# An attention stage keeps its logits negated and makes the left-block mask a GpSimd select

## The chip, the cores and the metric

The program runs on one core of a Trainium2 chip. The metric is the device time of one execution in microseconds (us), as a median over runs. The engines are named as in the profile: PE is TensorE (PEld its weight load), DVE is VectorE, ACT is ScalarE, POOL is GpSimd, and SP is the engine that issues most loads. L1017 is line 1017 of the kernel before.

## The reference, cut to what matters

Two layers act on a residual stream of 1024 tokens by 1024 channels in float32. The first is a gated MLP with a causal spatial gate over chunks of 128 tokens. The second, to which the change belongs, is sliding-window attention with 16 query heads, 4 shared key and value heads, a bias by distance, and one sink logit per head. A block of 128 queries sees its own block of keys and the one to its left:

```python
def block_fn(args):                      # one block of 128 queries
    i, qb = args
    ...
    logits = jnp.einsum('btkgd,bskd->bkgts', qb, kb).astype(jnp.float32) + alibi
    valid = in_window & ((start - BLOCK + c) >= 0)
    logits = jnp.where(valid, logits, -jnp.inf)
    m = jnp.maximum(jnp.max(logits, axis=-1), sink)
    p = jnp.exp(logits - m[..., None])
    denom = jnp.sum(p, axis=-1) + jnp.exp(sink - m)
    o = jnp.einsum('bkgts,bskd->btkgd', p.astype(vb.dtype), vb).astype(jnp.float32)
    o = o / denom.transpose(0, 3, 1, 2)[..., None]
```

The window is 128 keys, so of the left block a query in row r sees the columns above r, and of its own block the columns up to r. Each query therefore sees exactly 128 keys, one per column index.

## The kernel before

The tokens are worked in two halves of 512. Float32 products are made of three passes: each operand is split into a rounded part (`hi`, a copy on ScalarE, L105) and the rest (`lo`, a subtraction on VectorE, L106), and `mm3` (L167 to L170) issues the three matmuls. Weights are loaded by SP into a ring of three `raw` buffers, some are multiplied by a gain on GpSimd (L140), and then split; `wnext` takes the weight that is due and splits the one behind it, so that a weight is split one tile before its use.

Attention is cut into units: a unit is one block of 128 queries (`b`), one pair of key heads (`p`) and two of the four query heads that share each (`gp`), so four heads of 128 by 128 in a unit, and 16 units in each half. `attn` runs over them, with three stages of three units in flight. In one step it issues `scores` of unit i, `values` of unit i - 2, `transposes` of unit i - 1, some filler, `normalise` of unit i, and filler again. The filler is weight products of other phases: in the first call the projections for z, for keys and values and for q of the second half, in the second call the rest of z and the output projection.

`scores` makes the logits in PSUM (matmuls L997 and L1003). As each query sees one key per column index, the two blocks are merged into one row of 128 logits: a predicated copy with the mask `mrg` (L1008) takes those of the left block where the column is above the row; in the first block (b of 0) it takes -1e30. `tensor_tensor_reduce` (L1013) adds the bias, multiplies by a power of four (the weights of q carry its inverse), writes `pr` to SBUF and leaves the row maximum, begun at the sink logit, in `mx`. The sink logit itself stands as column 129 of `pr` (L986). `nm` is minus the maximum (L1017), and four exps on ScalarE (L1019) use it as their bias and sum their rows into `dn`.

`normalise` inverts `dn` and multiplies (L1025, L1026). `transposes` turns the four tiles on TensorE into the PSUM bank `pt` (L1032). ScalarE copies it to `pc` (L1035), and GpSimd clears in `pc` what does not belong to the unit's own block (an affine select in place, L1036). For b above 0 VectorE multiplies the same PSUM bank by the 0/1 mask `mprev` into `pp`, the left block's part (L1039). `values` multiplies `pc` with the values of the block (L1050) and `pp` with those of the left block (L1053), for two head pairs in turn, into `o`; VectorE multiplies by the gate (`yt`, L1057), which is split into q's place (L1059, helper lines L105 and L106, tiles `q_hi` and `q_lo`).

The pool of these tiles has one buffer for each tag unless it says otherwise. `pr`, `mx`, `nm` and `dn` have two. `pc` has one. `pp` and `yt` share the tag `pp`, and so one buffer, in turn.

The framework plans the order of instructions on each engine and sets the semaphores. An engine runs its own instructions strictly in the planned order, which need not be the order of the source.

Of the kernel before, what the change touches and what calls it, by code (L numbers as in the profile page):

```python
# [7 lines left out]
F32 = mybir.dt.float32  # L8
# [3 lines left out]
AF = mybir.ActivationFunctionType  # L12
ALU = mybir.AluOpType

P = 128
# [15 lines left out]
C_ID, C_BIAS, C_MERGE, C_PREV, C_QS = 0, 128, 640, 768, 896  # L31
# [19 lines left out]
def tile_yoco(  # L51
# [19 lines left out]
    nc = tc.nc  # L71
# [9 lines left out]
    def bank(tag, name):  # L81
        return psum.tile([P, 512], F32, tag=tag, name=name)
# [814 lines left out]
    bp = ctx.enter_context(tc.tile_pool(name="bp", bufs=1))  # L897
    bias = bp.tile([P, 4, P], F32, name="bias")
    nc.sync.dma_start(out=bias.rearrange("p a b -> p (a b)"), in_=consts[:, C_BIAS:C_BIAS + 512])
    mrg = bp.tile([P, P], F32, name="mrg")  # L900
    nc.sync.dma_start(out=mrg, in_=consts[:, C_MERGE:C_MERGE + P])
    mprev = bp.tile([P, P], F32, name="mprev")
    nc.sync.dma_start(out=mprev, in_=consts[:, C_PREV:C_PREV + P])
    neg = bp.tile([P, P], F32, name="neg")
    nc.vector.memset(neg, -1e30)

# [3 lines left out]
    nc.sync.dma_start(out=qsc, in_=consts[:, C_QS:C_QS + 2])  # L910
    snk = bp.tile([P, 4, 4], F32, name="snk")
    nc.sync.dma_start(out=snk.rearrange("p a b -> p (a b)"), in_=sinks.partition_broadcast(P))
    half = [slice(0, 64), slice(64, P)]
    vt = big.tile([P, NB, 256], F32, tag="P1_1", name="vt")

# [59 lines left out]
    class Unit:  # L975
# [4 lines left out]
        def scores(self):  # L980
            b, p, gp, q = self.b, self.p, self.gp, self.q
            bs_ = slice((b % 4) * P, (b % 4 + 1) * P)
            w0 = 0 if b > 0 else P
            pr = bp.tile([P, 4, P + 1], F32, tag="pr", name=f"pr{self.id}", bufs=2)
            mx = bp.tile([P, 2, 2], F32, tag="mx", name=f"mx{self.id}", bufs=2)
            nc.vector.tensor_copy(pr[:, :, P].rearrange("p (a b) -> p a b", a=2),  # L986
                                  snk[:, 2 * p:2 * p + 2, 2 * gp:2 * gp + 2])
            pss = []
            for par in range(2):
                pss.append(bank("s", f"s{self.id}_{par}").rearrange("p (g s) -> p g s", g=2))  # L990
            ks = slice(b * P - P + w0, (b + 1) * P)


            for g in range(2):
                m = p * 4 + gp * 2 + g
                for par in range(2):
                    nc.tensor.matmul(pss[par][:, g, w0:256], lhsT=q[par][:, m, bs_], rhs=kh[par][:, p, ks],  # L997
                                     start=g == 0, stop=False, skip_group_check=True)
            for g in range(2):
                m = p * 4 + gp * 2 + g  # L1000
                for par in range(2):
                    rw = half[par]
                    nc.tensor.matmul(pss[par][:, g, w0:256], lhsT=q[par][rw, m, bs_], rhs=kl[rw, p, ks],  # L1003
                                     start=False, stop=g == 1, skip_group_check=True)
            for par in range(2):
                ps = pss[par]
                c = ps[:, :, P:256]
                nc.vector.copy_predicated(c, mrg.bitcast(U32).unsqueeze(1).broadcast_to([P, 2, P]),  # L1008
                                          ps[:, :, 0:P] if b > 0 else neg.unsqueeze(1).broadcast_to([P, 2, P]))
                kv = 2 * p + par  # L1010
                for g in range(2):
                    gg = 2 * gp + g
                    nc.vector.tensor_tensor_reduce(pr[:, 2 * par + g, 0:P], c[:, g], bias[:, gg], 4.0 ** -kv,  # L1013
                                                   snk[:, kv, gg:gg + 1], ALU.add, ALU.max, mx[:, par, g:g + 1])
            nm = bp.tile([P, 2, 2], F32, tag="nm", name=f"nm{self.id}", bufs=2)
            dn = bp.tile([P, 2, 2], F32, tag="dn", name=f"dn{self.id}", bufs=2)
            nc.vector.tensor_scalar(nm, mx, -1.0, None, ALU.mult)  # L1017
            for i in range(4):
                nc.scalar.activation(pr[:, i], pr[:, i], AF.Exp, bias=nm[:, i // 2, i % 2:i % 2 + 1],  # L1019
                                     accum_out=dn[:, i // 2, i % 2:i % 2 + 1])  # L1020
            self.pr, self.dn = pr, dn

# [6 lines left out]
        def transposes(self):  # L1029
            pt = bank("s", f"pt{self.id}")  # L1030
            for i in range(4):
                nc.tensor.transpose(pt[:, i * P:(i + 1) * P], self.pr[:, i, 0:P], ident)  # L1032
            ptv = pt.rearrange("p (a b) -> p a b", a=4)
            self.pc = pc = bp.tile([P, 4, P], F32, tag="pc", name=f"pc{self.id}")
            nc.scalar.activation(pc, ptv, AF.Copy)  # L1035
            nc.gpsimd.affine_select(pc, pc, [[0, 4], [1, P]], ALU.is_ge, 0.0, base=0, channel_multiplier=-1)  # L1036
            if self.b > 0:
                self.pp = bp.tile([P, 4, P], F32, tag="pp", name=f"pp{self.id}")
                nc.vector.tensor_tensor(self.pp, ptv, mprev.unsqueeze(1).broadcast_to([P, 4, P]), ALU.mult)  # L1039

        def values(self):
            b, p, gp, q, z = self.b, self.p, self.gp, self.q, self.z
# [186 lines left out]
```

## Time and profile before

| what | us |
| --- | --- |
| median of 3 runs (lowest, highest) | 1073.43 (1072.39, 1078.94) |
| the profiled execution, its time | 1077.21 |
| the profiled execution, its span from first to last instruction | 1075.5 |

The profile covers one execution. Busy time of an engine does not count issue, waiting or semaphores; matmuls overlap one another and their weight loads. A window gives the busy time of each engine in a stretch of the span, and the clock that TensorE was granted there as a share of full speed. In a timeline a row can stand for several like instructions in a row (x2, x4), and the brackets give the idle time of the engine before it and what ended it.

### The profile page before, as it was taken

What the parts mean: (1) busy time and instruction counts of PE and PEld (TensorE: products, weight loads), DVE (VectorE), ACT (ScalarE), POOL (GpSimd) and SP (SyncE); (2) the same over time, 40 slices, a digit from 0 to 9 for tenths busy, and PEclk for the clock granted to TensorE, in tenths of its full rate; (3) what the DMA queues carried; (4) which work ended last, traced back from release to release, by engine and by line L of the source; (5) the groups of instructions that cost most, each with busy time, mean ns of one, the idle gap of its engine ahead of it and who ended that gap; (6) DMA issues with size and microseconds to landing.
All of it is one profiled execution on the core that took longest, in us unless ns stands there. A gap on an engine that the chain in (4) does not pass through costs nothing.

```text
span 1075.5 us, 14187 instructions
## 1 busy us (share of the span) xinstructions
PE 1051.4 (98%) x5108; PEld 859.1 (80%) x5108; DVE 781.6 (73%) x1335; ACT 582.7 (54%) x983; POOL 282.3 (26%) x199
## 2 busy tenths in 40 slices
PE   9999999999999999999999999999999989999997
PEld 7887778888888888888878878788778767777775
DVE  6987456867767767767795896746768985778873
ACT  7684444555565565555445464536675455675631
POOL 0000023254253443531561211313212323200120
PEclk9999999999999999999999999999999999999999
DMA  8787243334334333448968633724111212112353
GB/s 299 267 274 261 96 158 107 117 117 139 113 108 139 126 117 113 145 142 281 353 239 289 195 118 105 263 98 157 59 59 60 79 53 85 59 59 79 119 176 117
DMA packets 68709, 159.75 MB, mean 149 GB/s; under 512 B 6176, under 2 KB 16800, under 8 KB 68640
## 3 DMA queue, kind: packets, MB, share of 16 engines
q1 hardware_dynamic: 63744, 150.37, 41.0%
q10 hardware_dynamic: 4896, 8.48, 2.2%
q8 instruction: 40, 0.66, 0.3%
q14 instruction: 29, 0.24, 0.1%
HBM read 127.37 MB, written 31.46 MB: 148 GB/s over the span
## 4 chain that ended last, share of the span: by engine, by line
PE 79%; DVE 11%; ACT 3%; issue 2%; DMA 2%; POOL 2%; DVEq 0%; POOLq 0%; ACTq 0%
PE ub L168 5%; PE ub L170 5%; PE ub L169 5%; PE ob L168 5%; PE ob L169 5%; PE ob L170 5%; PE qz L168 4%; PE qz L170 4%; PE qz L169 4%; PE uc L168 3%; PE uc L170 3%; PE uc L169 3%; PE sp L592 3%; PE vb L168 2%; PE vb L169 2%
## 5 line engine op out<-in xcount | busy, mean ns | idle before, releaser
L140 POOL TENSOR_TENSOR raw_w<-raw_w,gn 128x1024 f32<-128x1024 f32 x32 | 66.4, 2076 | 186.2 <-DMA raw_w<-in_wqz_dram 164.7
L168 PE MATMUL qz<-n_hi,whi 128*128 128x512 f32 x256 | 102.8, 402 | 0.1
L170 PE MATMUL qz<-n_hi,wlo 128*128 128x512 f32 x256 | 100.8, 394 | 1.2 <-DVE wlo L106 1.2
L169 PE MATMUL qz<-n_lo,whi 128*128 128x512 f32 x256 | 100.4, 392 | 0.0
L106 DVE TENSOR_TENSOR wlo<-raw_w,whi 128x1024 fp32r<-128x1024 f32 x40 | 57.7, 1443 | 32.0 <-ACT whi L105 28.7
L1036 POOL TENSOR_SCALAR_AFFINE_SELECT pc<-pc 128x512 f32<-128x512 f32 x32 | 24.9, 779 | 151.9 <-ACT pc L1035 151.9
L105 ACT ACTIVATE whi<-raw_w 128x1024 fp32r<-128x1024 f32 x40 | 42.2, 1055 | 34.6 <-PE qz L169 15.4
L105 ACT ACTIVATE uzhilo_g<-f 128x1024 fp32r<-128x1024 f32 x31 | 32.9, 1060 | 50.0 <-PE uc L170 42.6
L170 PEld LDWEIGHTS qz<-n_hi,wlo 128*128 128x128 f32 x256 | 48.4, 189 | 11.9 <-DVE wlo L106 1.6
L168 PEld LDWEIGHTS qz<-n_hi,whi 128*128 128x128 f32 x256 | 48.5, 189 | 10.8 <-ACT pr L1019 0.4
L169 PEld LDWEIGHTS qz<-n_lo,whi 128*128 128x128 f32 x256 | 48.6, 190 | 9.5
L106 DVE TENSOR_TENSOR uzhilo_g<-f,uzhilo_g 128x1024 fp32r<-128x1024 f32 x31 | 39.0, 1257 | 21.9 <-ACT uzhilo_g L105 21.9
L205 POOL TENSOR_TENSOR f<-raw_uz,raw_uz 128x512 f32<-128x512 f32 x16 | 21.5, 1343 | 125.3 <-DVE uzhilo_g L106 125.3
L1019 ACT ACTIVATE pr<-pr,nm 128x129 f32<-128x129 f32 x128 | 49.8, 392 | 8.0 <-DVE nm L1017 5.4
L205 POOL TENSOR_TENSOR f<-raw_uz 128x512 f32<-128x512 f32 x16 | 20.6, 1291 | 126.6 <-DMA raw_uz<-in_wuz_in_dram 71.7
L208 ACT ACTIVATE uz_slots<-ub 128x512 f32<-128x512 f32 x48 | 28.4, 591 | 43.6 <-PE ub L170 41.5
L168 PE MATMUL ub<-T,whi_g 128*128 128x512 f32 x128 | 50.6, 396 | 0.0
L168 PE MATMUL ub<-T,uzhilo_g 128*128 128x512 f32 x128 | 50.5, 394 | 0.0
L170 PE MATMUL ub<-T,wlo_g 128*128 128x512 f32 x128 | 49.9, 390 | 0.0
L170 PE MATMUL ub<-T,uzhilo_g 128*128 128x512 f32 x128 | 49.9, 390 | 0.0
L169 PE MATMUL ub<-T,whi_g 128*128 128x512 f32 x128 | 49.8, 389 | 0.0
L169 PE MATMUL ub<-T,uzhilo_g 128*128 128x512 f32 x128 | 49.8, 389 | 0.0
(316 smaller groups left out, 3287.7 us busy)
## 6 DMA issues: line engine op xcount, KB each, us to landing
raw_uz<-in_wuz_in_dram SPq DMA_DIRECT2D x32, 512.0 KB, 3.5
raw_w<-in_wqz_dram SPq DMA_DIRECT2D x32, 512.0 KB, 3.5
td<-uz_slots SPq DMA_DIRECT2D x56, 256.0 KB, 2.0
orawP2a<-td SPq DMA_DIRECT2D x28, 512.0 KB, 4.5
raw<-in_wv_in_dram SPq DMA_DIRECT2D x17, 512.0 KB, 4.9
orawP2b<-in_wo_a_dram SPq DMA_DIRECT2D x17, 512.0 KB, 6.2
vg<-vd SPq DMA_DIRECT2D x8, 1024.0 KB, 5.4
raw_o<-in_wo_a_dram SPq DMA_DIRECT2D x15, 512.0 KB, 5.4
```

The source lines that it names most:

```text
L105: nc.scalar.activation(hi, src, AF.Copy)
L106: nc.vector.tensor_tensor(lo, src, hi.bitcast(F32), ALU.subtract)
L140: nc.gpsimd.tensor_tensor(rv, rv, g, ALU.mult)
L168: nc.tensor.matmul(out, lhsT=a_hi, rhs=b_hi, start=start, stop=False, skip_group_check=True)
L169: nc.tensor.matmul(out, lhsT=a_hi, rhs=b_lo, start=False, stop=False, skip_group_check=True)
L170: nc.tensor.matmul(out, lhsT=a_lo, rhs=b_hi, start=False, stop=stop, skip_group_check=True)
L205: (eng or nc.vector).tensor_tensor(out, a, b, op)
L208: nc.scalar.activation(out, a, AF.Copy)
L592: nc.tensor.matmul(psv[:, n], lhsT=d["vg"][:, 4 * j + n, i * P:(i + 1) * P], rhs=d["wc"], start=True, stop=True)
L1019: nc.scalar.activation(pr[:, i], pr[:, i], AF.Exp, bias=nm[:, i // 2, i % 2:i % 2 + 1], accum_out=dn[:, i // 2, i % 2:i % 2 + 1])
L1036: nc.gpsimd.affine_select(pc, pc, [[0, 4], [1, P]], ALU.is_ge, 0.0, base=0, channel_multiplier=-1)
```

## The change

The sinks are multiplied by -1 once, when they are loaded. `tensor_tensor_reduce` multiplies by minus the power of four and reduces with the minimum, so that `pr`, its sink column and `mx` hold negated logits. The exps take a factor of -1 and `mx` itself as bias; the negation into `nm` is gone from each unit, and its tile too. The mask `mprev` and its load are gone. In place of VectorE's product from PSUM, GpSimd makes `pp` by an affine select from `pc`, the copy in SBUF, ahead of the in-place select that clears the rest of `pc`.

```diff
-    mprev = bp.tile([P, P], F32, name="mprev")
-    nc.sync.dma_start(out=mprev, in_=consts[:, C_PREV:C_PREV + P])
...
+    nc.vector.tensor_scalar(snk, snk, -1.0, None, ALU.mult)
...
-                    nc.vector.tensor_tensor_reduce(pr[:, 2 * par + g, 0:P], c[:, g], bias[:, gg], 4.0 ** -kv,
-                                                   snk[:, kv, gg:gg + 1], ALU.add, ALU.max, mx[:, par, g:g + 1])
-            nm = bp.tile([P, 2, 2], F32, tag="nm", name=f"nm{self.id}", bufs=2)
+                    nc.vector.tensor_tensor_reduce(pr[:, 2 * par + g, 0:P], c[:, g], bias[:, gg], -(4.0 ** -kv),
+                                                   snk[:, kv, gg:gg + 1], ALU.add, ALU.min, mx[:, par, g:g + 1])
             dn = bp.tile([P, 2, 2], F32, tag="dn", name=f"dn{self.id}", bufs=2)
-            nc.vector.tensor_scalar(nm, mx, -1.0, None, ALU.mult)
             for i in range(4):
-                nc.scalar.activation(pr[:, i], pr[:, i], AF.Exp, bias=nm[:, i // 2, i % 2:i % 2 + 1],
+                nc.scalar.activation(pr[:, i], pr[:, i], AF.Exp, bias=mx[:, i // 2, i % 2:i % 2 + 1], scale=-1.0,
                                      accum_out=dn[:, i // 2, i % 2:i % 2 + 1])
...
             nc.scalar.activation(pc, ptv, AF.Copy)
-            nc.gpsimd.affine_select(pc, pc, [[0, 4], [1, P]], ALU.is_ge, 0.0, base=0, channel_multiplier=-1)
             if self.b > 0:
                 self.pp = bp.tile([P, 4, P], F32, tag="pp", name=f"pp{self.id}")
-                nc.vector.tensor_tensor(self.pp, ptv, mprev.unsqueeze(1).broadcast_to([P, 4, P]), ALU.mult)
+                nc.gpsimd.affine_select(self.pp, pc, [[0, 4], [-1, P]], ALU.is_ge, 0.0, base=-1, channel_multiplier=1)
+            nc.gpsimd.affine_select(pc, pc, [[0, 4], [1, P]], ALU.is_ge, 0.0, base=0, channel_multiplier=-1)
```

## Rows read from the trace of the kernel before

**Rows 1.** The page, part 1: busy us of an engine, its share of the span, and its instructions.

```profile
PE 1051.4 (98%) x5108; PEld 859.1 (80%) x5108; DVE 781.6 (73%) x1335; ACT 582.7 (54%) x983; POOL 282.3 (26%) x199
```

**Rows 2.** Windows by stage: the stretch and its length, then busy us of each engine (with the number of its instructions), the granted clock, the share of the DMA engines and GB/s. The first is the first attention call with the rest of its filler, the second the second call.

```profile
745.00:890.00 145.00, 139.03 (x776) 109.04 (x775) 113.10 (x309) 90.82 (x222) 38.34 (x30) 0.99 0.22 70
...
905.00:1035.00 130.00, 130.00 (x709) 100.11 (x707) 101.24 (x309) 83.82 (x215) 23.15 (x22) 1.00 0.28 93
```

**Rows 3.** Windows of 5 us within the first attention call, with the same columns (PE, PEld, DVE, ACT, POOL, clock, DMA share, GB/s).

```profile
860.00:865.00 5.00, 3.11 (x18) 2.25 (x18) 3.47 (x9) 4.56 (x12) 0.16 (x1) 0.90 0.00 0
865.00:870.00 5.00, 5.00 (x18) 3.96 (x18) 4.70 (x17) 1.97 (x9) 0.64 (x1) 0.76 0.20 56
...
880.00:885.00 5.00, 3.88 (x20) 2.70 (x21) 4.18 (x8) 4.77 (x13) 0.96 (x1) 1.00 0.01 3
```

**Rows 4.** Waits of TensorE from 640 us to the end: who waited for whom, us in total, times, the longest.

```profile
PE pt L1032 <- DVE pr L1026: 3.2, 3, 1.9
PE o L1053 <- DVE pp L1039: 2.0, 2, 1.7
```

**Rows 5.** Views of one line or tile each, the row of its instructions: count, then nanoseconds of one (least, median, most), first and last start, and the shapes.

```profile
L1036 POOL TENSOR_SCALAR_AFFINE_SELECT pc<-pc x32: 637/637/1609, 756.5 to 1029.4; 128x512 f32<-128x512 f32 x32
...
L1039 DVE TENSOR_TENSOR pp<-pt,mprev x28: 676/691/692, 767.7 to 1031.2; 128x512 f32<-128x512 f32 x28
...
L1017 DVE TENSOR_SCALAR nm<-mx x32: 153/161/1765, 751.3 to 1022.1; 128x4 f32<-128x4 f32 x32
...
L1013 DVE CUSTOM_DVE_ANT_0 pr<-s,bias,snk x128: 337/347/353, 750.1 to 1021.4; 128x128 f32<-128x128 f32 x128
...
L1026 DVE TENSOR_TENSOR pr<-pr,dn x32: 678/692/1589, 753.4 to 1026.6; 128x512 f32<-128x512 f32 x32
...
L106 DVE TENSOR_TENSOR q_lo<-yt,q_hi x32: 410/426/855, 767.2 to 1038.4; 128x256 fp32r<-128x256 f32 x32
```

**Rows 6.** Groups by line and shape on VectorE, 745 to 1040 us: count, busy us, mean nanoseconds of one, idle time before them.

```profile
L1026 DVE TENSOR_TENSOR pr<-pr,dn 128x512 f32<-128x512 f32 x32 | 23.7, 740 | 0.9
...
L1039 DVE TENSOR_TENSOR pp<-pt,mprev 128x512 f32<-128x512 f32 x28 | 19.3, 688 | 0.6
...
L1017 DVE TENSOR_SCALAR nm<-mx 128x4 f32<-128x4 f32 x32 | 10.5, 328 | 0.1
```

**Rows 7.** The timeline around 858 to 863 us: start, us, engine, line, operation.

```profile
858.26 1.90 POOL L140 TENSOR_TENSOR raw_w<-raw_w,gn 128x1024 f32<-128x1024 f32 x1 [2.70 <-DVE mx L1013]
858.42 1.76 DVE L1017 TENSOR_SCALAR nm<-mx 128x4 f32<-128x4 f32 x1
858.54 0.42 ACT L105 ACTIVATE q_hi<-yt 128x256 fp32r<-128x256 f32 x1 [2.40 <-DVE yt L1057]
...
860.28 0.40 ACT L1019 ACTIVATE pr<-pr,nm 128x129 f32<-128x129 f32 x1 [1.32 <-DVE pr L986]
...
863.01 0.41 PE L1032 MATMUL pt<-ident,pr 128*128 128x128 f32 x2 [1.89 <-DVE pr L1026]
```

**Rows 8.** The timeline of five units: the q_lo subtraction of the unit before on VectorE, and TensorE's value products (L1050 from pc, L1053 from pp); for the first of them also the pc select on GpSimd.

```profile
801.00 0.91 POOL L1036 TENSOR_SCALAR_AFFINE_SELECT pc<-pc 128x512 f32<-128x512 f32 x1 [11.90 <-ACT pc L1035]
...
801.00 0.42 DVE L106 TENSOR_TENSOR q_lo<-yt,q_hi 128x256 fp32r<-128x256 f32 x1
...
801.96 0.43 PE L1050 MATMUL o<-pc,vt 128*64 128x256 f32 x1 [0.19 <-POOL pc L1036]
...
841.79 0.41 DVE L106 TENSOR_TENSOR q_lo<-yt,q_hi 128x256 fp32r<-128x256 f32 x1
...
842.81 0.61 PE L1050 MATMUL o<-pc,vt 128*64 128x256 f32 x2
...
850.93 0.43 DVE L106 TENSOR_TENSOR q_lo<-yt,q_hi 128x256 fp32r<-128x256 f32 x1 [0.33 <-ACT q_hi L105]
...
851.14 0.65 PE L1050 MATMUL o<-pc,vt 128*64 128x256 f32 x2
...
852.13 0.43 PE L1053 MATMUL o<-pp,vt 128*64 128x256 f32 x1 [0.35 <-DVE pp L1039]
...
878.67 0.65 PE L1050 MATMUL o<-pc,vt 128*64 128x256 f32 x2
...
879.80 0.41 DVE L106 TENSOR_TENSOR q_lo<-yt,q_hi 128x256 fp32r<-128x256 f32 x1
...
880.99 0.43 PE L1053 MATMUL o<-pp,vt 128*64 128x256 f32 x1 [1.67 <-DVE pp L1039]
...
987.33 0.42 DVE L106 TENSOR_TENSOR q_lo<-yt,q_hi 128x256 fp32r<-128x256 f32 x1
...
987.77 0.43 PE L1050 MATMUL o<-pc,vt 128*64 128x256 f32 x1
```

**Rows 9.** The timeline of GpSimd: the weight multiply that follows the pc select in two of these units.

```profile
838.82 1.90 POOL L140 TENSOR_TENSOR raw_w<-raw_w,gn 128x1024 f32<-128x1024 f32 x1
...
848.54 1.90 POOL L140 TENSOR_TENSOR raw_w<-raw_w,gn 128x1024 f32<-128x1024 f32 x1
```

**Rows 10.** The timeline of VectorE where the sink logits come in (the copies into pr of the first two units, and the next instruction).

```profile
652.44 0.24 DVE L986 COPY pr<-snk 128x4 f32<-128x4 f32 x2 [2.29 <-DMA snk<-in_sinks_dram]
654.72 1.29 DVE L106 TENSOR_TENSOR n_lo<-nt,n_hi 128x512 fp32r<-128x512 f32 x2 [2.04 <-ACT n_hi L105]
```

## The prediction, made before the change was run

> **What bounds the kernel now.** I read the page's busy shares first: TensorE is busy 1051.4 of 1075.5 us, VectorE 781.6 [rows 1]. So work taken from another engine pays only where TensorE stands idle. The windows by stage say where the change can reach: the first attention call with what is left of its filler (745 to 890 us) has TensorE busy 139.0 of 145.0, so 6.0 us idle at a mean granted clock of 0.99; the second call (905 to 1035 us) has it busy in all 130.0 [rows 2]. The fine windows of the first call show where the 6.0 us lie: 1.89 us in 860 to 865, 1.12 us in 880 to 885, and behind the first of these the granted clock reads 0.90 and 0.76 [rows 3], a mixture of the 2.4 GHz level with some time at 1.2. Those two stretches cost 5 x 0.10 + 5 x 0.24 = 1.7 us of clock. The pause of 1.67 us at 879 to 881 [rows 8] left the clock at 1.00 [rows 3]. The waits of TensorE name two releasers that the change touches: pt (the transposes) on pr, 3.2 us in 3 waits, and o (the value products) on pp, 2.0 us in 2 [rows 4].
>
> **The change, part by part.** VectorE loses nm, 32 x 0.328 = 10.5 us, and pp, 28 x 0.688 = 19.3 us: 29.8 us in all, of which a unit loses 0.16 + 0.69 = 0.85 us at the medians [rows 5, 6]. As TensorE is the bound, this is not the gain.
>
> Removing nm takes a link out of maximum, nm, exp. Its median is 0.161 us, its longest 1.765 [rows 5]. The long ones are waits: at 858.42 nm ran until 860.18, while GpSimd's weight multiply ran from 858.26 to 860.16; the first exp began at 860.28, and the transposes at 863.01 after 1.89 us of idle TensorE [rows 7]. Without nm the first exp follows the q_hi copy on ScalarE, which ends at 858.96: 1.3 us earlier, so are the transposes, and 1.89 - 1.3 leaves a pause of 0.6, shorter than the 1.67 that cost no clock. **Term 1: -1.3 us; term 2: -1.7 us of clock.** Ends of both together: 0, if the sink copy or q_lo that stand behind nm are held in its place and something needs them; and -7.7, if all idle time (6.0) and the clock (1.7) come back. I take -3.0, since only this wait hangs on nm alone.
>
> The select for pp on GpSimd: the shape is that of the pc select, min and median 0.637, longest 1.609 [rows 5]; nothing in the tensor differs but the pattern, so I take 0.64. It cannot start with the ScalarE copy alone. pp and yt share one buffer (tag pp, one deep), so it also waits for the last reader of the unit before's yt, the q_lo subtraction on VectorE. That held for VectorE's pp too; new is that the in-place pc select stands behind it in GpSimd's queue. Formerly pc was ready early, and the four pc products could run before pp was there. Now both come at q_lo's end + 0.05 (a handoff such as from 801.91, the end of the select, to the product at 801.96) + 2 x 0.64 = 1.33 us. Of the 28 units with a left block five are then late by VectorE's old times: q_lo ends at 801.42, 842.20, 851.36, 880.21 and 987.75, their products began at 801.96, 842.81, 851.14, 878.67 and 987.77 [rows 8], so 0.79 + 0.72 + 1.55 + 2.87 + 1.31 = 7.2 us. Two of these already waited 0.35 and 1.67 for pp [rows 8], which leaves 5.2. The other 23 come out in time, their cover being the filler's weight products between the copy and the value products. VectorE's 0.85 us relief stands ahead of q_lo; taken off each, 0, 0, 0.35, 0.35 and 0.46 remain. **Term 3: +1.2 us**, ends 0 and +5.2. Behind the waiting select on GpSimd stands the next weight multiply: in the unit of 842 it ran at 838.82, in that of 851 at 848.54 [rows 9]; behind a select pair that ends at 843.53 and 852.69 they would come 4.7 and 4.1 us later, and ScalarE's split of that weight after them. I cost this at nothing, because weights are split one tile ahead of use; without that cover it is up to 8.8 us.
>
> The lock: nm (0.153 to 1.765), pr's normalisation (0.678 to 1.589) and q_lo (0.410 to 0.855) sometimes run long; the old pp, which read PSUM, never did (0.676 to 0.692) [rows 5]. So work that is never held moves to the engine that holds others, 28 x 0.64 = 17.9 us of it. The Trainium skill (SBUF — State Buffer, Who interferes with whom) states that a VectorE instruction with two SBUF inputs contends with a GpSimd instruction that reads SBUF, and that the later one is blocked for the whole of the first. The trace agrees in which rows run long. By that rule at its fullest the relief shrinks from 29.8 to 11.9 us, and the sum turns to no gain (rival below). Sized by rows: the normalisation's mean is 0.740 against a minimum of 0.678 [rows 5, 6] with 32 selects about, so 0.06 us each; on the path it matters in the 3 waits for pr. **Term 4: +0.2 us**, ends 0 and 3 x 0.64 = 1.9.
>
> The negation of the sinks adds one VectorE instruction of 16 elements a row, once, between 0.15 us (the smallest small-tile row, nm) and 1.77 (nm held). It stands where VectorE waits 2.29 us for the sinks and then 2.04 us for ScalarE [rows 10]: 0, and without that cover its own length. One load on SP goes, ahead of that of the sinks, and gates nothing else. Exp with a factor of -1 and the reduction by minimum have the shapes of before; the trace has no row with a factor or a minimum there, and a cost either way is bounded by the spread of the existing row, 0.337 to 0.353 over 128 of them [rows 5], 2 us of VectorE: 0 on the path.
>
> The sum: -1.3 - 1.7 + 1.2 + 0.2 = -1.6 us. The profiled execution took 1077.21 us (span 1075.5 and 1.7 around it), so 1075.6. It lies 3.78 above the median of the three runs, 1073.43; against that I forecast 1071.8.
>
> **The rivals.** (a) The select pair on GpSimd comes late and the waiting moves there. For it: the five late units; against it: 23 units have room and VectorE runs ahead. Price: +5.2 with nothing of terms 1 and 2 gained, 1078.6; with the two delayed weight multiplies coming through in full +14.0, 1087.4. It decides over 1% (10.7 us) from 0.38 us of lateness in each of 28 units. (b) The lock eats the relief: term 4 at its end of 1.9 and term 3 without the relief's help in the two units that waited already (2 x 0.85 = 1.7 more), so -3.0 + 2.9 + 1.9 = +1.8, 1075.2; for it speak the long rows, against it the small mean. This is the page's rule named above. (c) All idle time of the first call and its clock come back: -7.7, 1065.7. For it: in 840 to 885 VectorE is the engine that TensorE waits for; against it: part of the idle time hangs on ScalarE's exps and on q_lo. (d) The change does not do what it says: the instructions are planned in another order on the engines (the order is not that of the source: the sink copies of the first two units ran at 652.44 [rows 10], far ahead of their scores), and this outweighs it. Its size has no row; I give it a gain over 1% only, losses being in (a).
>
> **How the numbers follow.** Forecast 0.47, from 0 to -4 us; (a) 0.22, of which 0.08 beyond +10.7; (b) 0.13; (c) 0.15; (d) 0.03. The predicted time is the forecast's. The range goes from (c), 1065, to beyond (a)'s first price, 1081; it leaves out (a)'s tail, (d) and some of the stretch between, under 0.2. The forecast's own range is 1069 to 1074. About 1% is what a measurement of this kernel can tell from no change: faster 0.03 is (d), slower 0.08 is (a)'s tail, the rest is within.
>
> **What would show it.** Right: the wait of pt on pr in the first call falls below 2 us and no window of 860 to 870 shows a clock under 0.95; VectorE's busy time falls by 25 to 30 us, GpSimd's rises by 18 to 22; o waits on GpSimd (pc or pp) in two to five units for 1 to 3 us. Wrong: o waiting on GpSimd for more than 5 us, the second call no longer at full TensorE, weight multiplies starting later and ScalarE's split waiting for them (a); the normalisation's mean over 0.9 us (b); all idle time gone (c); another order of the filler on TensorE (d).

## The result, and the profile after

| | before | after |
| --- | --- | --- |
| median of the runs, us (lowest, highest) | 1074.72 (1072.39, 1078.94), 14 runs | 1079.93 (1077.11, 1086.08), 14 runs |
| the profiled execution, its time, us | 1077.21 | 1077.78 |
| its span, us | 1075.5 | 1076.0 |

The ratio is 1.0048, 95% interval 1.0035 to 1.0061: the change costs 5.2 us (3.8 to 6.6). The forecast was a gain of 1.6 us. The time lies inside the range and within 1%, but on the other side of no change.

One caution for reading the two profiles: that of before lies 2.5 us above its median, that of after 2.2 below, so their spans differ by 0.5 us only. What follows is read from the attention stretch. From the first score product to the last value product it took 287.9 us before (746.78 to 1034.70) and 291.1 after (744.78 to 1035.85), which is 3.2 us more, with TensorE idle 6.0 and 11.3 us of it.

The page of after, part 1 (busy us, share, instructions), to be read against [rows 1]:

```profile
PE 1047.3 (97%) x5108; PEld 855.7 (80%) x5108; DVE 765.3 (71%) x1276; ACT 581.6 (54%) x983; POOL 304.0 (28%) x227
```

GpSimd rose by 21.7 us. VectorE fell by 16.3 only, though the instructions taken from it had held 29.8. The windows of after, in the columns of [rows 2]:

```profile
745.00:890.00 145.00, 135.12 (x765) 106.36 (x764) 103.27 (x280) 90.33 (x222) 47.33 (x41) 0.99 0.18 66
905.00:1035.00 130.00, 128.54 (x700) 99.19 (x698) 93.57 (x278) 83.08 (x216) 35.36 (x39) 1.00 0.26 93
```

TensorE's idle time grew from 6.0 to 9.9 us in the first call and from 0 to 1.5 in the second: 5.4 us together. The waits of TensorE from 640 us to the end, those that answer to [rows 4], tell who ended it:

```profile
PE o L1048 <- POOL pc L1037: 10.2, 7, 2.7
PE pt L1030 <- DVE pr L1024: 1.1, 2, 0.8
```

The value products now wait for `pc` on GpSimd, 10.2 us in 7 waits, where before they waited 0.2 us for `pc` and 2.0 for `pp`. Transposes wait 1.1 instead of 3.2. Net, the waits grew by 10.0 - 2.0 - 2.1 = 5.9 us, near the 5.3 by which idle time grew. They are not the whole account, as the stretch grew by 3.2 only. Most of the rest is in the value products themselves, which were busy for less time after. The busy time of TensorE on the tile `o`, first before and then after:

```profile
740.00:1050.00 310.00, 35.88 (x240) 0.99 0.26 86
740.00:1050.00 310.00, 34.04 (x240) 0.99 0.24 84
```

The step from these 3.2 us to the 5.2 of the medians can only be estimated. Both profiled executions have a mean granted clock of 0.997; over all runs it is 0.9944 after, and 0.9958 in the 78 runs of the kernel before beside the experiments. The difference is about 1.5 us of the span. So on the mean after lost more clock, which the two profiles don't show.

Who is waited for on the other engines, 745 to 1040 us, after:

```profile
POOL pp L1036 <- DVE q_lo L106: 97.5, 20, 9.2
...
ACT pr L1017 <- DVE mx L1012: 33.2, 19, 4.1
...
ACT pc L1033 <- PE pt L1030: 25.0, 13, 4.4
```

and the same view of before for ScalarE:

```profile
ACT pc L1035 <- PE pt L1032: 41.6, 22, 4.2
...
ACT pr L1019 <- DVE nm L1017: 5.4, 5, 1.9
```

Two things are to be seen. In 20 of its 28 units GpSimd's new select starts when `q_lo` releases the shared buffer, not when ScalarE's copy is there. And ScalarE waits at another place: before, mostly for the transposes ahead of the `pc` copy (22 times), rarely for `nm` ahead of the exps (5); after, 19 times for the maximum ahead of the exps. Its planned order has changed. Of the 28 steps that have all three, the `pc` copy and `q_hi` mostly run ahead of the exps before (27 and 24 times); after, `q_hi` runs behind the exps in all 28 and the `pc` copy in 18. VectorE followed: `q_lo` comes ahead of the step's normalisation 25 times before and 7 after. The order on TensorE is nearly the same.

One step of after shows the whole chain, in the timeline from 866 to 873 us (start, us, engine, line, operation, idle time before it):

```profile
866.62 0.40 ACT L1017 ACTIVATE pr<-pr,mx 128x129 f32<-128x129 f32 x1 [1.27 <-DVE mx L1012]
...
867.49 1.90 POOL L140 TENSOR_TENSOR raw_w<-raw_w,gn 128x1024 f32<-128x1024 f32 x1 [6.14 <-DMA raw_w<-in_wqz_dram]
867.60 1.82 DVE L985 COPY pr<-snk 128x4 f32<-128x4 f32 x1
...
868.18 0.40 ACT L105 ACTIVATE q_hi<-yt 128x256 fp32r<-128x256 f32 x1
...
869.52 0.69 DVE L1024 TENSOR_TENSOR pr<-pr,dn 128x512 f32<-128x512 f32 x1
870.13 0.42 DVE L106 TENSOR_TENSOR q_lo<-yt,q_hi 128x256 fp32r<-128x256 f32 x1
...
870.47 1.22 DVE L106 TENSOR_TENSOR wlo<-raw_w,whi 128x1024 fp32r<-128x1024 f32 x1
...
870.68 1.50 POOL L1036 TENSOR_SCALAR_AFFINE_SELECT pp<-pc 128x512 f32<-128x512 f32 x1 [1.30 <-DVE q_lo L106]
...
872.25 0.63 POOL L1037 TENSOR_SCALAR_AFFINE_SELECT pc<-pc 128x512 f32<-128x512 f32 x1
...
872.94 1.13 PE L1048 MATMUL o<-pc,vt 128*64 128x256 f32 x4 [2.15 <-POOL pc L1037]
```

The exps go first on ScalarE, so `q_hi` comes behind them. On VectorE the sink copy is held for 1.82 us beside GpSimd's weight multiply, as `nm` was before [rows 7], and the normalisation stands ahead of `q_lo`. `q_lo` ends at 870.55, `pp` is selected (held for 1.50, beside VectorE's split of a weight), then `pc`, and TensorE has stood still for 2.15 us. From these rows the shares can be estimated: `q_hi` was there at 868.58, so `q_lo` is 1.55 us late. Without the hold the normalisation would have followed the last exp (its sum is read by 868.28) and ended near 869.1; that makes 0.5 by its place and 1.0 by the held copy. The held select adds 1.50 - 0.63 = 0.87.

Two more of the seven waits show what else made the pair late:

```profile
816.68 0.42 DVE L106 TENSOR_TENSOR q_lo<-yt,q_hi 128x256 fp32r<-128x256 f32 x1
816.90 1.96 POOL L140 TENSOR_TENSOR raw_w<-raw_w,gn 128x1024 f32<-128x1024 f32 x1 [4.97 <-DVE pr L1024]
818.82 0.63 POOL L1036 TENSOR_SCALAR_AFFINE_SELECT pp<-pc 128x512 f32<-128x512 f32 x1
819.51 0.63 POOL L1037 TENSOR_SCALAR_AFFINE_SELECT pc<-pc 128x512 f32<-128x512 f32 x1
820.20 0.66 PE L1048 MATMUL o<-pc,vt 128*64 128x256 f32 x4 [1.46 <-POOL pc L1037]
...
843.47 0.42 DVE L106 TENSOR_TENSOR q_lo<-yt,q_hi 128x256 fp32r<-128x256 f32 x1
844.01 1.23 DVE L106 TENSOR_TENSOR wlo<-raw_w,whi 128x1024 fp32r<-128x1024 f32 x1
844.02 1.72 POOL L1036 TENSOR_SCALAR_AFFINE_SELECT pp<-pc 128x512 f32<-128x512 f32 x1 [1.30 <-DVE q_lo L106]
845.80 0.70 POOL L1037 TENSOR_SCALAR_AFFINE_SELECT pc<-pc 128x512 f32<-128x512 f32 x1
846.56 0.66 PE L1048 MATMUL o<-pc,vt 128*64 128x256 f32 x4 [2.73 <-POOL pc L1037]
```

In the first, a weight multiply stands ahead of the pair in GpSimd's queue; in the second, the select is held for 1.72 us beside the split of a weight. The seven value products that waited began at 784.87, 803.88, 820.20, 846.56, 872.94, 936.11 and 1028.11, and the time from the end of `q_lo` to them was 1.85, 1.91, 3.10, 2.68, 2.39, 1.52 and 2.73 us, where two selects at 0.64 and a handoff would be 1.33.

The fine windows of after, columns of [rows 3]:

```profile
845.00:850.00 5.00, 3.44 (x21) 2.59 (x22) 4.89 (x15) 2.33 (x7) 2.56 (x3) 1.00 0.29 105
...
865.00:870.00 5.00, 5.00 (x27) 4.08 (x25) 4.85 (x14) 3.23 (x11) 1.90 (x1) 1.00 0.25 97
870.00:875.00 5.00, 2.85 (x15) 1.24 (x12) 4.85 (x14) 1.51 (x3) 2.13 (x2) 0.75 0.27 105
875.00:880.00 5.00, 5.00 (x23) 4.25 (x24) 2.85 (x7) 2.56 (x10) 2.14 (x2) 0.91 0.00 0
```

The pause at 860 to 863 is gone and its loss of clock too, but the new pause brings one back: 5 x 0.25 + 5 x 0.09 = 1.7 us, as much as before. The longest pause, 2.73 us up to 846.56, cost no clock.

The rows of one line or tile each, after, with count and least, median and longest nanoseconds, beside [rows 5]:

```profile
L985 DVE COPY pr<-snk x32: 135/164/1816, 650.2 to 1015.9; 128x4 f32<-128x4 f32 x32
...
L1036 POOL TENSOR_SCALAR_AFFINE_SELECT pp<-pc x28: 630/635/1715, 767.4 to 1032.4; 128x512 f32<-128x512 f32 x28
```

and two groups on VectorE, 745 to 1040 us, in the columns of [rows 6]:

```profile
L1024 DVE TENSOR_TENSOR pr<-pr,dn 128x512 f32<-128x512 f32 x32 | 24.3, 761 | 0.9
...
L985 DVE COPY pr<-snk 128x4 f32<-128x4 f32 x30 | 13.1, 438 | 0.5 <-PE pt L1030 0.5
```

The sink copy's mean was 0.176 us before (5.3 us for the 30 copies): it grew by 7.8 us. `nm` had stood 5.3 us above its median (10.5 - 32 x 0.161), so as much as its hold, and some more, is found again here.

### The profile page after: what moved, and what is told of

Read it like the earlier page. It is cut to its first block, busy times and chain, and to the rows that moved or that the text cites. A ratio compares the mean times of both kernels' runs of the same rounds, so it can differ in the third digit from the quotient of the medians.

```text
span 1076.0 us, 14195 instructions
## 1 busy us (share of the span) xinstructions
PE 1047.3 (97%) x5108; PEld 855.7 (80%) x5108; DVE 765.3 (71%) x1276; ACT 581.6 (54%) x983; POOL 304.0 (28%) x227
## 4 chain that ended last, share of the span: by engine, by line
PE 81%; DVE 9%; ACT 4%; POOL 2%; issue 2%; DMA 1%; SPq 0%; POOLq 0%; DVEq 0%; ACTq 0%
PE ub L170 5%; PE ub L168 5%; PE ub L169 5%; PE ob L168 5%; PE ob L169 5%; PE ob L170 5%; PE qz L168 4%; PE qz L169 4%; PE qz L170 4%; PE uc L170 3%; PE uc L169 3%; PE uc L168 3%; PE sp L592 3%; PE vb L169 2%; PE vb L170 2%
## 5 line engine op out<-in xcount | busy, mean ns | idle before, releaser
L1017 ACT ACTIVATE pr<-pr,mx 128x129 f32<-128x129 f32 x128 | 50.0, 393 | 33.4 <-DVE mx L1012 33.2
L1036 POOL TENSOR_SCALAR_AFFINE_SELECT pp<-pc 128x512 f32<-128x512 f32 x28 | 23.0, 822 | 123.5 <-DVE q_lo L106 97.5
```

The source lines that it names most:

```text
L1017: nc.scalar.activation(pr[:, i], pr[:, i], AF.Exp, bias=mx[:, i // 2, i % 2:i % 2 + 1], scale=-1.0, accum_out=dn[:, i // 2, i % 2:i % 2 + 1])
L1036: nc.gpsimd.affine_select(self.pp, pc, [[0, 4], [-1, P]], ALU.is_ge, 0.0, base=-1, channel_multiplier=1)
```

## The experiments

Four theories were open after the result. **Order:** without `nm` the plan of ScalarE changes (exps first), and this makes `pc` and `q_lo` late. **Shared buffer:** the `pp` select waits in GpSimd's queue for the buffer that `yt` holds until `q_lo`, and the `pc` select stands behind it. **Negation:** negated logits cost something themselves. **Lock:** more work on GpSimd holds VectorE, or is held by it. Ratios are to the kernel before, run beside each on the same chip, with 95% intervals.

**The negation alone** (the mask stays on VectorE):

```diff
+    nc.vector.tensor_scalar(snk, snk, -1.0, None, ALU.mult)
...
-            nc.vector.tensor_scalar(nm, mx, -1.0, None, ALU.mult)
...
-                nc.scalar.activation(pr[:, i], pr[:, i], AF.Exp, bias=nm[:, i // 2, i % 2:i % 2 + 1],
+                nc.scalar.activation(pr[:, i], pr[:, i], AF.Exp, bias=mx[:, i // 2, i % 2:i % 2 + 1], scale=-1.0,
```

> One part of the change alone: logits negated and nm gone, pp still VectorE's product from PSUM. The plan of ScalarE is the one of the full change (exps, then q_hi, then the pc copy). Theory O (the lost time needs both parts: without nm the planner puts the exps of a unit ahead of the pc copy and of q_hi, which makes both some 2 us later, and the two selects on GpSimd in a row then come too late): -2 to +1.5 us against before, since the pc copy had 4 to 5 us of room and VectorE's pp does not hold pc back; TensorE's wait of o on GpSimd's pc stays under 2 us. Theory B (the selects and the shared buffer alone, whatever ScalarE's order): -1 to -3 us. Theory N (the order of ScalarE alone costs it): +4 to +6 us.

Measured: 1074.37 us, ratio 0.9978 (0.9964 to 0.9993), -2.4 us. Waits of TensorE from 745 us on, and the window of the first call:

```profile
PE o L1052 <- DVE pp L1038: 1.7, 3, 0.7
PE o L1049 <- POOL pc L1035: 1.3, 2, 1.1
PE pt L1031 <- DVE pr L1025: 0.3, 1, 0.3
```

```profile
745.00:890.00 145.00, 141.91 (x791) 111.27 (x791) 110.63 (x298) 92.31 (x224) 39.56 (x30) 1.00 0.21 73
```

The wait for `pr` falls from 3.2 to 0.3, the clock in this window is 1.00, idle time halves to 3.1. So the negation gains by itself, although its ScalarE order is that of after, exps first. The gain is a little above the range that the order theory gave. Outside this stretch the profiled execution did lose clock (0.73 at 635 to 640 us and 0.92 at 640 to 645), as much as before lost at 860 to 870 [rows 3].

**The select alone** (`nm` stays):

```diff
-                nc.vector.tensor_tensor(self.pp, ptv, mprev.unsqueeze(1).broadcast_to([P, 4, P]), ALU.mult)
+                nc.gpsimd.affine_select(self.pp, pc, [[0, 4], [-1, P]], ALU.is_ge, 0.0, base=-1, channel_multiplier=1)
+            nc.gpsimd.affine_select(pc, pc, [[0, 4], [1, P]], ALU.is_ge, 0.0, base=0, channel_multiplier=-1)
```

> The other part alone: pp as a select on GpSimd from pc, logits and nm as before. The plan of ScalarE is the one of before (pc copy, q_hi, exps). Theory O: +0 to +2.5 us against before, o waiting on GpSimd's pc for 2 to 5 us, as the five late units of the prediction say. Theory B: +5 to +7 us, o waiting on GpSimd for about 10 us as in the full change. Theory L (the lock between GpSimd and VectorE): +4 to +7 us with the normalisation's mean well above 0.74 us. Theory N: within 1 us of before.

Measured: 1079.92 us, ratio 1.0028 (1.0009 to 1.0047), +3.0 us. ScalarE keeps the order of before. Two waits, 745 to 1040 us:

```profile
POOL pp L1036 <- DVE q_lo L106: 65.8, 14, 10.0
...
PE o L1048 <- POOL pc L1037: 7.2, 5, 1.9
```

The select loses even in the old order, through `q_lo`, and by an amount between the ranges of the two theories. The parts add up to -2.4 + 3.0 = +0.6 us; together they cost 5.2. The rest, some 4.6 us (by the three intervals give or take 2.9), belongs to neither part alone.

**The full change with ScalarE's order held to `pc` copy, `q_hi`, exps:**

```diff
+        def exps(self):
...
+            if i < len(units):
+                with ExitStack() as s:
+                    if i > 0:
+                        s.enter_context(tc.issue_after(units[i - 1].ci))
+                    if i > 1:
+                        s.enter_context(tc.issue_after(units[i - 2].qi))
+                    units[i].exps()
```

> The full change with ScalarE's order pinned by plan-only edges to that of before: in each step the exps are issued behind the pc copy and q_hi. Theory O: the pc copy and q_lo are early again, o waits on GpSimd under 5 us, the time is 3 to 6 us below the full change, so -1 to +2 us against before. Theories B and L: as the full change, +4 to +6 us against before.

Measured: 1076.17 us, ratio 0.9997 (0.9983 to 1.0011). The wait for `pc` falls to 5.5 us in 3 (from 10.2 in 7), not quite under 5. The order is worth about 5.5 us here (0.9997 against 1.0048).

**The kernel before with the order of after, strictly:**

```diff
+                with ExitStack() as s:
+                    if i < len(units):
+                        s.enter_context(tc.issue_after(units[i].ei))
+                    units[i - 2].values()
...
+                with ExitStack() as s:
+                    if i >= 2:
+                        s.enter_context(tc.issue_after(units[i - 2].qi))
+                    units[i - 1].transposes()
```

> The kernel before with ScalarE's order pinned to that of the full change (exps, q_hi, pc copy); nothing else differs. Theory O: the order alone is mostly hidden by the 4 to 5 us of room of pc, 0 to +2.5 us against before. Theory N: +4 to +6 us. Theory B: within 1 us of before.

Measured: 1087.53 us, ratio 1.0105 (1.0082 to 1.0128), +11.3 us: far more than any theory gave it. ScalarE's exps wait for `nm`, with `q_hi`, the `pc` copy and the splits behind them (waits of ScalarE, 745 to 1040 us; before 5.4 us in 5):

```profile
ACT pr L1020 <- DVE nm L1018: 35.8, 13, 4.9
```

That this wait makes the 11.3 us is not shown. The planned order on TensorE changed too, far more than in after, and its value products were busy for 42.5 us here against 35.9 before. What the pin does on TensorE was not separated from what it does on ScalarE, so the run can't size the order in after.

**The kernel before with its own order pinned** (`pc` copy, `q_hi`, exps, by the lines of the pin above), a control:

> The kernel before with ScalarE's order pinned to pc copy, q_hi, exps in every step; its plan had that order in 25 or so of its 32 steps already. A control for the runs with the pin: if the pin's gain there (0.9953 for the negation with the pin against 0.9978 without) is one of order alone, this run falls too, by 1 to 3 us. If it needs the negation, within 1 us of before, as nm keeps the exps late anyway.

Measured: 1077.20 us, ratio 1.0004 (0.9986 to 1.0023). The pin itself costs and gains nothing clear of the noise; as the plan had this order in most steps already, it changes little here.

**The full change, with a buffer of its own for `yt`** (the constant -1e30 is kept as one column to make room, which changes no value):

```diff
-    neg = bp.tile([P, P], F32, name="neg")
+    neg = bp.tile([P, 1], F32, name="neg")
...
-            yt = bp.tile([P, 2, P], F32, tag="pp", name=f"yt{self.id}")
+            yt = bp.tile([P, 2, P], F32, tag="yt", name=f"yt{self.id}")
```

> The full change, but yt has a buffer of its own in place of sharing that of pp (room for it comes from keeping the constant of -1e30 as one column that is broadcast, used in the 2 x 4 units of the first block). pp's select then waits for the pc copy alone and not for q_lo of the unit before; ScalarE's order stays that of the full change. Theory S (the shared buffer makes the pair of selects late, and the order hurts because it makes q_lo late): GpSimd's wait on q_lo goes from 97.5 us to nothing, o waits on GpSimd under 3 us, and the time is 4 to 7 us below the full change: -2 to +1 us against before. Theory P (the late pc copy itself does it, with or without q_lo): +3 to +5 us against before.

Measured: 1072.56 us, ratio 0.9966 (0.9951 to 0.9982), -3.7 us, more than the shared-buffer theory forecast (-2 to +1). The one-column constant that comes with it is no cause: the eight copies that use it took 3.5 us after and 3.4 here. GpSimd's select now waits for ScalarE's copy, in no unit for `q_lo`:

```profile
POOL pp L1036 <- ACT pc L1033: 123.7, 24, 11.0
```

TensorE still waits 4.2 us for `pc` in 5 waits: the copy comes behind the exps.

**The select alone with that buffer:** the two diffs above together.

> The select part alone (nm kept, plan's order of before), with yt in its own buffer. Theory S: the buffer is what the select part lost by (it measured 1.0028 alone), so -1 to -4 us against before. If the select on GpSimd is itself the loss: +2 to +4 us, as without the buffer.

Measured: 1072.03 us, ratio 0.9975 (0.9958 to 0.9991), where the select alone gave 1.0028. The shared buffer is what the select alone lost by.

**The full change with the buffer and the pinned order:**

> The full change with both mends: yt in its own buffer, and ScalarE's order pinned to pc copy, q_hi, exps. Theory S: like the run with the buffer alone, -3 to 0 us against before. Theory P: no better than the pin alone, which measured 0.9997 of before: -1 to +1 us. If the lock between GpSimd's selects and VectorE costs what rival (b) said, neither mend goes below 0 us.

Measured: 1070.00 us, ratio 0.9939 (0.9921 to 0.9957), -6.6 us, beyond the forecast of -3 to 0. Its windows, columns of [rows 2]:

```profile
745.00:890.00 145.00, 143.00 (x809) 114.18 (x809) 109.71 (x287) 93.61 (x227) 46.98 (x42) 1.00 0.21 73
905.00:1035.00 130.00, 130.00 (x697) 100.00 (x696) 93.12 (x273) 78.16 (x207) 33.86 (x37) 1.00 0.29 102
```

and what is left of the waits that the change touches:

```profile
PE pt L1034 <- DVE pr L1028: 2.1, 4, 0.9
```

No value product waits for GpSimd, and 4.0 of the first call's 6.0 us of idle time and its loss of clock are back. Yet VectorE's holds are longer here than in either kernel (mean of the normalisation, columns of [rows 6]):

```profile
L1028 DVE TENSOR_TENSOR pr<-pr,dn 128x512 f32<-128x512 f32 x32 | 27.6, 863 | 1.0
```

This beats both kernels, before by 0.6% and, by the two ratios, after by 1.1%.

**The negation alone with the pinned order:**

> Negated logits without nm, pp on VectorE as before, ScalarE's order pinned to pc copy, q_hi, exps. It asks whether the gain of the negation alone (0.9978 of before) hangs on the order that comes with it. Theory S: no, with one select a unit and pp on VectorE pc has room in either order, -1 to -4 us against before. If the order of exps first was itself the gain: within 1 us of before.

Measured: 1071.40 us, ratio 0.9953 (0.9936 to 0.9970). That is -5.1 us, beyond the range of -1 to -4. Two things follow. The order costs something without the select too: 0.9978 with the exps first, 0.9953 without, 2.7 us, though hardly more than the noise of the two (give or take 2.4). And the run does not differ from the one above by more than the intervals: that the select on GpSimd adds to the negation, even with both mends, is not shown.

The ratios so far, side by side:

| | `nm` kept, order of before | negation, order of after | negation, order held |
| --- | --- | --- | --- |
| `pp` on VectorE | 1 | 0.9978 | 0.9953 |
| select on GpSimd, shared buffer | 1.0028 | 1.0048 | 0.9997 |
| select on GpSimd, buffer for `yt` | 0.9975 | 0.9966 | 0.9939 |

Down each column, the select with the shared buffer costs 0.3 to 0.7%, and with a buffer for `yt` it costs nothing; in the first column it gains 0.3%. From the second column to the third, the order costs 0.3% in the first and the last row and 0.5% where the buffer is shared.

**The same as the best version, with `pc` selected first:**

```diff
-            self.ci = nc.scalar.activation(pc, ptv, AF.Copy).ins
+            self.pp = pp = bp.tile([P, 4, P], F32, tag="pp", name=f"pp{self.id}") if self.b > 0 else pc
+            self.ci = nc.scalar.activation(pp, ptv, AF.Copy).ins
+            nc.gpsimd.affine_select(pc, pp, [[0, 4], [1, P]], ALU.is_ge, 0.0, base=0, channel_multiplier=-1)
...
+                nc.gpsimd.affine_select(pp, pp, [[0, 4], [-1, P]], ALU.is_ge, 0.0, base=-1, channel_multiplier=1)
```

> The version with both mends, and the two selects in the other order: ScalarE copies pt into pp's tile, GpSimd selects pc out of it first and clears pp in place second, so that the pc products wait for one select and not for two. If the pair still costs anything behind the mends: 0.5 to 2 us below the version with both mends (0.9939 of before). Theory S says that the pair now has room: the same as that version within 1 us.

Measured: 1069.24 us, ratio 0.9944 (0.9924 to 0.9963): the same. Once the pair does not wait for `q_lo`, which select goes first is worth nothing that these runs can tell.

**The kernel before with a second `pc` select on GpSimd** in the 28 units (it repeats the first and changes no value):

```diff
             nc.gpsimd.affine_select(pc, pc, [[0, 4], [1, P]], ALU.is_ge, 0.0, base=0, channel_multiplier=-1)
             if self.b > 0:
+                nc.gpsimd.affine_select(pc, pc, [[0, 4], [1, P]], ALU.is_ge, 0.0, base=0, channel_multiplier=-1)
+            if self.b > 0:
```

> The kernel before with the in-place pc select issued twice in the 28 units with a left block (the second changes nothing in the data), so that GpSimd runs as many selects as in the full change while pp, nm and all else stay; pc is ready 0.64 us later, inside its 4 to 5 us of room. Theory L (the added selects hold VectorE): +2 to +4 us against before, the normalisation's mean over 0.85 us. Theories S and O: within 1 us of before.

Measured: 1076.22 us, ratio 1.0005 (0.9990 to 1.0020). GpSimd's load of after in the order of before, without the wait for a buffer, costs nothing clear of the noise (at most 2.2 us by the interval):

```profile
PE pt L1032 <- DVE pr L1026: 2.9, 2, 1.9
PE o L1055 <- DVE pp L1041: 2.2, 2, 1.9
PE o L1052 <- POOL pc L1038: 1.1, 1, 1.1
```

Neither the lock nor the longer path of `pc` (one more select, 0.64 us) is the loss by itself.

## Why the prediction was wrong, step by step

**The step that failed is term 3.** It said +1.2 us for the late select pair, with +5.2 as its end, and measured 10.0 - 2.0 = +8.0 us by the waits. The mechanism was named rightly: the pair waits for `q_lo`, and `pc` stands behind `pp`. The size rested on three things that did not hold.

- It took `q_lo`'s times from the old profile. But the plan changed with the removal of `nm`: exps ahead of `q_hi` on ScalarE, normalisation ahead of `q_lo` on VectorE. Of its five late units only two (those of 801.96 and 842.81) are among the seven that waited.
- It set VectorE's relief of 0.85 us ahead of `q_lo`. In the step of after shown above the normalisation and a held sink copy stood there.
- It took 1.33 us from `q_lo` to the first product. In the seven units it was 1.52 to 3.10, in five of them with a select held beside VectorE and in one with a weight multiply ahead of the pair on GpSimd. The prediction asked what stands behind the selects, not what stands ahead of them. Had it been 1.33 in each, some 5.8 of the 10.2 us would not be there (an estimate: in each unit the smaller of its wait and of what exceeds 1.33).

The runs show the shared buffer as what makes the select cost anything: with a buffer for `yt` the change gains (0.9966), in the old order too (0.9975). The order makes it worse. With the order held the change stands at 0.9997, but this is no proof that the loss is gone, as the negation alone with that order gives 0.9953: the select still costs 4.7 us (give or take 2.4), and the negation pays for it.

The sum also lacked a gain and a loss: the value products, busy 1.8 us less, and the clock of the runs, where -1.7 us was forecast and the mean over the runs went the other way, by an estimated 1.5 us.

**Rival (a)** had the place right, o waiting on GpSimd and the second call no longer at full TensorE, and its first price, 5.2 us, is the measured cost. That agreement is luck: (a) priced five late units in the old order with nothing gained elsewhere; what happened were seven waits in a new order, with 2.1 us gained at the transposes and 1.8 in the value products, and with clock lost. Its tail, late weight multiplies that come through in full, did not come: the one wait of TensorE for a weight's split is 1.1 us after and 1.2 before.

**Rival (d)** was the real hole. It allowed another planned order, but looked for it on TensorE, gave it 0.03, and let it only gain. The order changed on ScalarE and VectorE, and it made the difference between a loss and none (1.0048 and 0.9997).

**Term 1** was right in its place: -2.1 us of waits for `pr` against -1.3 forecast, and -2.9 with the negation alone. **Term 2** was right for the pause that it named (865 to 870 reads 1.00) and wrong in the sum: the new pause of 2.15 us lost the same 1.7 us of clock later. With the negation alone the stretch lost no clock.

**Term 4 and rival (b).** The bound for (b), a normalisation over 0.9 us, was not reached: 0.761 against 0.740 before. The rule behind it, in the Trainium skill (SBUF — State Buffer, Who interferes with whom), says that of two instructions on VectorE and GpSimd that need their shared port pair, a VectorE copy in a two-port mode among them, the one issued later is blocked for the whole of the first. The traces agree: the hold of `nm` went to the next instruction in line, the sink copy, 1.816 us at its longest beside a weight multiply of 1.90, and its 7.8 us are the largest part of why VectorE's busy time fell by 16.3 and not by 25 to 30. As a cost of 28 more selects (b) is not borne out (1.0005), and the version with both mends is faster with a normalisation of 0.863. In after, though, the holds strike a chain that has no slack left: in the step shown they make some 1.9 of the 2.4 us that the chain was late. So, as far as these runs go, the holds cost where the shared buffer has taken the slack; the bound on the normalisation looked at the wrong instruction. How the 10.2 us divide exactly into order, holds and the weight multiply stays open.

**The costs at nothing.** The negation of the sinks took 0.17 us inside the wait for the sinks, as forecast, and the exps with a factor took 0.393 us on the mean against 0.392 before. GpSimd's rise of 21.7 us was inside the 18 to 22 forecast; the select's median, 0.635, was the 0.64 assumed, but its mean was 0.822 (23.0 us for 28), and five of the seven waits had a long one in them (0.97 to 1.72).

**Rival (c)**, all idle time and its clock back, priced 7.7 us. The version with both mends gained 6.6, the negation alone with the order held 5.1, so most of it was within reach without the select.

## What to carry to other kernels

An instruction moved to another engine brings its waits along: before moving it, list what it waits for beside its input (a shared buffer above all), and what stands behind it in the new queue. Removing a short instruction can turn the planned order on engines that the edit does not touch, so compare the orders of every engine before a sum on old times is believed, and give a changed order both signs. Price what stands ahead of it there too, and take a held instruction's long times and not its median where there is no slack. Where a part gains alone and the whole loses, run the parts and the mended whole, and compare each mend with the part under the same mend: here the whole with its order held looked free beside the kernel before, and was 0.4% behind the negation alone in that order.

## What the runs showed that was not expected

Fixing the order of three kinds of instruction on ScalarE, an engine busy 54% of the span, moved the kernel before by 11.3 us with no work added, and changed the order on TensorE with it. A copy of 4 elements a row on VectorE took up to 1.816 us, eleven times its median of 0.164, because it stood where `nm` had stood. The length of a pause of TensorE did not tell whether clock was lost: 1.89 us before was followed by windows at 0.90 and 0.76 [rows 3, 7], and 2.15 us after by 0.75 and 0.91, while 2.73 us in the same run of after left it at 1.00 (the window from 845 us). So the prediction's step from a shorter pause to a full clock had less behind it than its rows seemed to give.
